# Expert stage of a recurrent/attention/MoE block: weight splits emitted four ahead, products with the weight's high part first

## The chip, the cores and the metric

One NeuronCore of one Trainium2 chip runs the whole block. The metric is device time in microseconds for one execution of the program. The kernel before takes 1919.03 us (median of 3 runs, 1914.31 to 1919.47); the one execution that was profiled took 1921.2 us, of which the trace spans 1919.1 us.

## The reference, cut to what matters

The block is an RWKV branch, a differential attention branch, a mix of the two, then a mixture of experts, then a gated per-layer term. The change touches the experts alone. Each of 1024 tokens goes to 2 of 32 experts; an expert is

```python
def expert_block(args):
    xb, e = args
    return (jax.nn.silu(xb @ w_gate[e]) * (xb @ w_up[e])) @ w_down[e]
```

with `w_gate` and `w_up` of 1024x512 and `w_down` of 512x1024, all in 32-bit floats. So each expert brings 6 MiB of weights and meets at most 128 rows of tokens in the main pass (an overflow loop behind it takes what is over 128).

## The kernel before, in words

A product of two 32-bit operands is built from three matmuls on rounded parts: each operand is split into a high part (`fp32r`, a copy on ScalarE) and a low part (the difference, on VectorE), and `mm3` (L69 to L73) issues high x high, high x low of the right operand, low x high, one after the other for each 128 rows of the contraction. In the experts the left operand is the tokens (`exh`, `exl`) or the activated rows (`eah`, `eal`), and the right operand, 512 columns wide, is the weight (`ewh`, `ewl`).

**Weights.** `weight_order` lists 192 pieces of 1 MiB, six for an expert: the upper half of gate and of up, then the two halves of down of the expert before, then the lower halves of gate and up. `wdma` (L1024) loads a piece on SyncE's queue into a ring of nine raw buffers (`ewp` five, `md` four). `wload` splits it, `ewh` on ScalarE (L78) and `ewl` on VectorE (L79), into a ring of four pairs (`wsp`, n = 4). So piece n+4 reuses the pair of piece n, and a load reuses the raw buffer of the load nine before it. Nine pieces are loaded before the stage starts.

**Experts.** For expert e the loop of `experts` gathers the tokens of e+1 (GpSimd, L1074), runs the first halves of gate and up (`expert_up`, PSUM tiles `pg`, `pu`), then `expert_down` of expert e-1, then the transposes and split of the next tokens (`expert_x`, `tp4` at L1064), then the second halves, then `expert_act`: Silu on ScalarE (L1097) and a product on VectorE (L1098). `expert_down` transposes the activated rows, splits them into `eah`, `eal`, multiplies by down into two PSUM tiles `pey`, copies these on ScalarE (L1117) and scatters the rows (GpSimd, L1118). `weight()` is a generator's step: a piece's split is written into the program right ahead of the matmuls that read it. `between` puts steps of the overflow's index work after each expert from the third on.

**Order.** The program is written in the order above, but a planner (`schedule_with_timeline_sim=True`) lays each engine's instructions out by a simulated timeline, with the place in the program as priority; on the chip each engine's order is then fixed. That is why the rows show `pg`, `pu` and `pey` matmuls interleaved.

Of the kernel before, what the change touches and what calls it, by code (L numbers as in the profile page):

```python
# [25 lines left out]
AF = mybir.ActivationFunctionType  # L26
# [6 lines left out]
D = 1024  # L33
NT = S // 128
KT = D // 128
# [9 lines left out]
NE = 32  # L45
FF = 512
# [6 lines left out]
class Kern:  # L53
    def __init__(self, ctx, tc, A, out, dbg=None):
        self.ctx, self.tc, self.nc, self.A, self.out = ctx, tc, tc.nc, A, out
        self.dbg = dbg or {}
        self.ovat = NE - 1
        self.flush = (NE - 1,)
        self.pre, self.bigat = (0, 1, 1, 1, 1, 1, 2, 2), 1
        self.nhold = 4  # L60
        self.w2seq = "sog sol sog l ogy l l l l"
        self.atn, self.w1gap, self.w1n, self.fln = 2.6, 3, 1.5, 0.6
# [1035 lines left out]
        self.nc.vector.tensor_mul(ac, ac, P[1])  # L1098
        return ac

    def expert_down(self, ac, rid, ws):

        ah = self.et("ah", [128, 4, 128], F32R)
        al = self.et("al", [128, 4, 128], F32R)
        self.split(ah, al, self.tp4(ac, 0))
        y = self.et("ye", [128, D])
        k = 0
        for hi, lo in ws:
            kn = hi.shape[1]
            for b in range(2):  # L1110
                cs = slice(b * 512, (b + 1) * 512)
                for i in range(kn):
                    self.mm3(self.pey[b], ah[:, k + i, :], al[:, k + i, :], hi[:, i, cs], lo[:, i, cs],
                             start=(k + i == 0), stop=(k + i == 3))
            k += kn
        for b in range(2):
            self.nc.scalar.activation(y[:, b * 512:(b + 1) * 512], self.pey[b], AF.Copy)  # L1117
        return self.nc.gpsimd.indirect_dma_start(out=self.yd, out_offset=bass.IndirectOffsetOnAxis(ap=rid, axis=0),  # L1118
                                                 in_=y, in_offset=None, bounds_check=2 * S - 1, oob_is_err=False)

    def weight_order(self):

        up, down, order = [], [], []
        for e in range(NE):
            wg, wu, wd = self.weights(e)
            up.append([(w, k, 4, FF) for k in (0, 4) for w in (wg, wu)])
            down.append([(wd, k, 2, D) for k in (0, 2)])
        for e in range(NE):
            order += up[e][:2]
            if e and e - 1 not in self.flush:  # L1130
                order += down[e - 1]
            order += up[e][2:]
            if e in self.flush:
                order += down[e]
        return order

    def experts(self, raws, between):

        order = self.weight_order()
        hold = {}  # L1140
        load = lambda n: self.wdma(*order[n], after=hold.get(n), sync=True)
        raws = list(raws)
        done = 0

        def weight():
            nonlocal done
            if not raws:
                raws.append(load(done))
            done += 1
            return self.wload(*order[done - 1], raws.pop(0))  # L1150

        sent, prev = [], None

        def down():
            e, ac = prev
            st = self.expert_down(ac, self.ids[:, 0, e:e + 1], (weight() for _ in range(2)))
            for s in sent:
                self.tc.declare_no_dep(st.ins, s.ins, reason="rows of other assignments")
            sent.append(st)
            self.lasty = st  # L1160

        gather = lambda e: self.expert_gather(self.ids[:, 1, e:e + 1])
        x = None
        for e in range(NE):
            if x is None:
                xg = gather(e)
                if not e:
                    hold.update({n: self.lastx for n in range(len(raws), len(raws) + self.nhold)})
                x = self.expert_x(xg)
            P = self.pgu[e % 2]  # L1170
            ahead = e < NE - 1 and e not in self.flush
            if ahead:
                xg = gather(e + 1)
            self.expert_up(x, P, (weight() for _ in range(2)), 0)
            if prev is not None:
                down()
            nx = self.expert_x(xg) if ahead else None
            self.expert_up(x, P, (weight() for _ in range(2)), 4)
            x = nx
            prev = e, self.expert_act(P)  # L1180
            if e in self.flush:
                down()
                prev = None
            between(e)

    def overflow_loop(self):
        nc, tc, A = self.nc, self.tc, self.A
        n = nc.values_load(self.ebi[0:1, 16:17], min_val=0, max_val=15)
        with tc.For_i(0, n, 1) as i:  # L1189
            e = nc.values_load(self.ebi[0:1, bass.ds(i, 1)], engines=[mybir.EngineType.SP],  # L1190
                               min_val=0, max_val=NE - 1)
            nc.vector.tensor_copy(self.idc, self.ido[:, :, bass.ds(i, 1)].rearrange("p a b -> p (a b)"))
            wg, wu, wd = [A[nm][0, bass.ds(e, 1)].rearrange("o k n -> (o k) n") for nm in ("w_gate", "w_up", "w_down")]
            x = self.expert_x(self.expert_gather(self.idc[:, 1:2]))
            for k in range(0, KT, 2):
                self.expert_up(x, self.pgu[0], (self.wload(w, k, 2, FF, pre="o") for w in (wg, wu)), k)
            self.expert_down(self.expert_act(self.pgu[0]), self.idc[:, 0:1],
                             (self.wload(wd, k, 1, D, pre="o") for k in range(4)))


    def ple_proj(self, pool):
# [358 lines left out]
```

## Time and profile before

| | |
|---|---|
| median of 3 runs | 1919.03 us |
| the profiled execution | 1921.2 us, span 1919.1 us |
| expert stage, first to last expert matmul | from 1168.6 to about 1795 us of the span |
| TensorE busy over the span | 93% |
| VectorE, ScalarE, GpSimd busy | 70%, 45%, 15% |
| granted TensorE clock over the span | 0.970 |

Busy shares are averages over stages with different limits; the expert stage is read by itself, with the waits in it. Matmuls are pipelined: one lasts about 0.40 us, but the next one starts before its end, so the pace is the distance of the starts. "PE" is a matmul, "PEld" the load of its left operand, and "SPq" SyncE's queue of loads. A wait is named by the engine and line that waited and by what released it.

### The profile page before, as it was taken

What the parts mean: (1) busy time and instruction counts of PE and PEld (TensorE: products, weight loads), DVE (VectorE), ACT (ScalarE), POOL (GpSimd) and SP (SyncE); (2) the same over time, 40 slices, a digit from 0 to 9 for tenths busy, and PEclk for the clock granted to TensorE, in tenths of its full rate; (3) what the DMA queues carried; (4) which work ended last, traced back from release to release, by engine and by line L of the source; (5) the groups of instructions that cost most, each with busy time, mean ns of one, the idle gap of its engine ahead of it and who ended that gap; (6) DMA issues with size and microseconds to landing.
All of it is one profiled execution on the core that took longest, in us unless ns stands there. A gap on an engine that the chain in (4) does not pass through costs nothing. (4 is left out here: it accounts for less than half of the span.)

```text
span 1919.1 us, 28589 instructions
## 1 busy us (share of the span) xinstructions
PE 1792.2 (93%) x10864; PEld 1486.9 (77%) x10864; DVE 1347.0 (70%) x2578; ACT 858.7 (45%) x1241; POOL 297.2 (15%) x211
## 2 busy tenths in 40 slices
PE   6999999999999988999988996999999999999598
PEld 6999898898766667888866875777777777777487
DVE  6455867743788937666555778998888787888673
ACT  5244444421333312122222226777767767777432
POOL 0311211000332310101042001222211121120000
PEclk9999999999999988899989997999999999999799
DMA  6432242237676565445354448999999999999641
GB/s 216 128 116 85 76 129 95 82 120 258 200 246 229 192 230 184 135 157 178 122 193 128 168 174 298 353 366 371 337 335 351 353 343 349 334 334 337 256 179 44
DMA packets 241789, 421.39 MB, mean 220 GB/s; under 512 B 38769, under 2 KB 115697, under 8 KB 240754
## 3 DMA queue, kind: packets, MB, share of 16 engines
q1 hardware_dynamic: 194546, 346.12, 52.8%
q10 hardware_dynamic: 37888, 56.64, 8.1%
q0 software_dynamic: 9216, 16.80, 2.4%
q8 instruction: 86, 1.41, 0.3%
q14 instruction: 53, 0.43, 0.1%
HBM read 346.07 MB, written 90.18 MB: 227 GB/s over the span
## 5 line engine op out<-in xcount | busy, mean ns | idle before, releaser
L79 DVE TENSOR_TENSOR ewl<-ewp,ewh 128x2048 fp32r<-128x2048 f32 x108 | 245.6, 2287 | 51.4 <-ACT ewh L78 50.9
L71 PE MATMUL pj<-whi,hh 128*128 128x256 f32 x832 | 239.8, 288 | 0.3 <-ACT pjev L208 0.3
L72 PE MATMUL pj<-wlo,hh 128*128 128x256 f32 x832 | 239.2, 288 | 0.0
L73 PE MATMUL pj<-whi,hl 128*128 128x256 f32 x832 | 237.4, 286 | 0.0
L79 DVE TENSOR_TENSOR ewl<-md,ewh 128x2048 fp32r<-128x2048 f32 x84 | 191.3, 2286 | 36.9 <-ACT ewh L78 36.5
L78 ACT ACTIVATE ewh<-ewp 128x2048 fp32r<-128x2048 f32 x108 | 204.6, 1910 | 11.4 <-PE pg L73 5.7
L71 PEld LDWEIGHTS pj<-whi,hh 128*128 128x128 f32 x832 | 159.2, 191 | 7.7 <-issue 6.6
L78 ACT ACTIVATE ewh<-md 128x2048 fp32r<-128x2048 f32 x84 | 159.1, 1911 | 11.5 <-PE pu L73 5.6
L72 PEld LDWEIGHTS pj<-wlo,hh 128*128 128x128 f32 x832 | 159.2, 191 | 6.2 <-issue 5.3
L73 PEld LDWEIGHTS pj<-whi,hl 128*128 128x128 f32 x832 | 159.0, 191 | 2.6 <-issue 2.3
L1074 POOL DMA_INDIRECT xg<-h2d,ids x32 | 64.0, 2000 | 402.0 <-PE ptp L1064 368.4
L72 PE MATMUL pu<-ewl,exh 128*128 128x512 f32 x256 | 105.1, 411 | 17.2 <-DVE ewl L79 17.2
L71 PE MATMUL pu<-ewh,exh 128*128 128x512 f32 x256 | 103.2, 403 | 3.6 <-ACT ewh L78 3.6
L72 PE MATMUL pey<-ewl,eah 128*128 128x512 f32 x256 | 100.8, 401 | 5.8 <-DVE ewl L79 5.8
L71 PE MATMUL pg<-hh,whi 128*128 128x512 f32 x256 | 105.2, 411 | 0.0
L72 PE MATMUL pg<-ewl,exh 128*128 128x512 f32 x256 | 103.0, 402 | 2.0 <-DVE ewl L79 2.0
L72 PE MATMUL pg<-hl,whi 128*128 128x512 f32 x256 | 103.9, 406 | 0.0
L71 PE MATMUL pg<-ewh,exh 128*128 128x512 f32 x256 | 103.2, 403 | 0.6 <-ACT ewh L78 0.6
L73 PE MATMUL pg<-hh,wlo 128*128 128x512 f32 x256 | 102.4, 400 | 0.0
L73 PE MATMUL pg<-ewh,exl 128*128 128x512 f32 x256 | 101.3, 396 | 0.0
L73 PE MATMUL pu<-ewh,exl 128*128 128x512 f32 x256 | 101.0, 394 | 0.0
L73 PE MATMUL pey<-ewh,eal 128*128 128x512 f32 x256 | 97.6, 396 | 0.2 <-DVE eal L79 0.2
(455 smaller groups left out, 4269.1 us busy)
## 6 DMA issues: line engine op xcount, KB each, us to landing
ewp<-in_w_down_dram SPq DMA_DIRECT2D x42, 1024.0 KB, 7.2
ewp<-in_w_gate_dram SPq DMA_DIRECT2D x33, 1024.0 KB, 7.3
ewp<-in_w_up_dram SPq DMA_DIRECT2D x33, 1024.0 KB, 7.9
md<-in_w_up_dram SPq DMA_DIRECT2D x31, 1024.0 KB, 7.4
md<-in_w_gate_dram SPq DMA_DIRECT2D x31, 1024.0 KB, 7.5
md<-in_w_down_dram SPq DMA_DIRECT2D x22, 1024.0 KB, 7.0
wraw<-in_w_in_dram SPq DMA_DIRECT2D x42, 512.0 KB, 4.0
gd<-pjev ACTq DMA_DIRECT2D x32, 256.0 KB, 4.8
```

What stands on the lines that cost most here:

```text
L71: mm(ps, lh, rh, start=start, stop=False)
L72: mm(ps, lh, rl, start=False, stop=False)
L73: mm(ps, ll, rh, start=False, stop=stop)
L78: a = nc.scalar.activation(hi, src, AF.Copy)
L79: b = nc.vector.tensor_tensor(lo, src, hi.bitcast(F32), op=OP.subtract)
L1074: self.lastx = self.nc.gpsimd.indirect_dma_start(out=xg, out_offset=None, in_=self.h2d, in_offset=bass.IndirectOffsetOnAxis(ap=tid, axis=0 ...
```

## The change

The split of a piece, and the load that feeds it, are now written four pieces ahead: four before the loop, then one (`more()`) after the matmuls of each piece. Inside a piece the matmuls with its high part (eight, tokens' high and low part in turn) come first, and the four with its low part last; in `expert_down` both column halves do their high products before the low ones. `expert_down` is cut in three: `expert_rows` (transposes and split of the activated rows) now stands between the first half of gate and the first half of up; the products stand where they were; `expert_out` (copies and scatter) stands after the second half of gate. Silu follows gate's second half at once. The order of the pieces and of their loads, the ring sizes and the number of matmuls are as before.

```diff
+        def more():
+            nonlocal done
+            if done < len(order):
+                raw = raws.pop(0) if raws else load(done)
+                ready.append(self.wload(*order[done], raw))
+                done += 1
+
+        def up(x, P, i, k0):
+            hi, lo = ready.pop(0)
+            mm = self.nc.tensor.matmul
+            for j in range(4):
+                for z in range(2):
+                    mm(P[i], x[z][:, k0 + j, :], hi[:, j, :], start=(k0 + j + z == 0), stop=False)
+            for j in range(4):
+                mm(P[i], x[0][:, k0 + j, :], lo[:, j, :], start=False, stop=(k0 + j == KT - 1))
+            more()
...
+        x = self.expert_x(xg)
+        for _ in range(4):
+            more()
         for e in range(NE):
...
-            self.expert_up(x, P, (weight() for _ in range(2)), 0)
-            if prev is not None:
-                down()
-            nx = self.expert_x(xg) if ahead else None
-            self.expert_up(x, P, (weight() for _ in range(2)), 4)
+            up(x, P, 0, 0)
+            if e:
+                a = self.expert_rows(ac)
+            up(x, P, 1, 0)
+            if e:
+                down(a)
+            nx = self.expert_x(xg) if e < NE - 1 else None
+            up(x, P, 0, 4)
+            ac = self.et("ac", [128, FF])
+            self.nc.scalar.activation(ac, P[0], AF.Silu)
+            if e:
+                out(e - 1)
+            up(x, P, 1, 4)
+            self.nc.vector.tensor_mul(ac, ac, P[1])
             x = nx
```

The products of down, with `a` the pair of split rows (`a[0]` high, `a[1]` low):

```diff
-        for hi, lo in ws:
-            kn = hi.shape[1]
-            for b in range(2):
-                cs = slice(b * 512, (b + 1) * 512)
-                for i in range(kn):
-                    self.mm3(self.pey[b], ah[:, k + i, :], al[:, k + i, :], hi[:, i, cs], lo[:, i, cs],
-                             start=(k + i == 0), stop=(k + i == 3))
-            k += kn
+        for b in range(2):
+            for i in range(kn):
+                for z in range(2):
+                    mm(self.pey[b], a[z][:, k + i, :], hi[:, i, half(b)], start=(k + i + z == 0), stop=False)
+        for b in range(2):
+            for i in range(kn):
+                mm(self.pey[b], a[0][:, k + i, :], lo[:, i, half(b)], start=False, stop=(k + i == 3))
```

## Rows read from the trace of the kernel before

**Rows 1.** Busy time by stage; columns: window, length, engines, clock, DMA share, GB/s.

```profile
1165.00:1345.00 180.00, 174.04 (x794) 139.96 (x795) 158.48 (x151) 132.88 (x112) 41.05 (x19) 0.98 0.99 358
1345.00:1790.00 445.00, 417.80 (x1909) 329.94 (x1907) 359.79 (x245) 317.38 (x270) 80.42 (x43) 1.00 0.96 341
...
1547.60:1626.90 79.30, 74.02 (x338) 58.49 (x337) 63.77 (x40) 57.04 (x49) 14.60 (x9) 1.00 0.97 344
```

**Rows 2.** Waits from 1345 to 1790 us: total us, times, longest.

```profile
DVE ewl L79 <- ACT ewh L78: 71.1, 55, 3.4
ACT eah L78 <- PE ptp L1064: 43.1, 22, 5.5
ACT eye L1117 <- PE pey L73: 34.5, 26, 2.8
ACT exh L78 <- PE ptp L1064: 31.6, 21, 3.9
PEld pu L72 <- DVE ewl L79: 24.2, 21, 1.8
...
PEld pey L72 <- DVE ewl L79: 9.1, 10, 1.8
...
PEld pg L72 <- DVE ewl L79: 5.0, 11, 1.3
...
PEld pey L71 <- ACT eah L78: 1.9, 3, 0.9
...
PEld pg L71 <- ACT ewh L78: 1.0, 1, 1.0
```

**Rows 3.** ScalarE's waits from 1165 to 1345 us.

```profile
ACT ewh L78 <- PE pu L73: 10.6, 15, 1.3
ACT ewh L78 <- PE pg L73: 10.4, 10, 3.8
```

**Rows 4.** Waits of SyncE's queue, 1200 to 1790 us.

```profile
SPq L1024 <- DVE ewl L79: 463.2, 164, 6.8
```

**Rows 5.** TensorE in order of time: a piece without a stall, then its end.

```profile
1375.01 0.40 PE L71 MATMUL pu<-ewh,exh 128*128 128x512 f32 x1
...
1377.81 0.60 PE L1064 MATMUL ptp<-ident,eac 128*128 128x128 f32 x4
```

**Rows 6.** TensorE in order of time: transposes, then a stall.

```profile
1494.51 0.60 PE L1064 MATMUL ptp<-ident,eac 128*128 128x128 f32 x4
1494.86 0.47 PE L71 MATMUL pu<-ewh,exh 128*128 128x512 f32 x1
1496.45 0.50 PE L72 MATMUL pu<-ewl,exh 128*128 128x512 f32 x1 [1.12 <-DVE ewl L79]
1496.79 0.40 PE L73 MATMUL pu<-ewh,exl 128*128 128x512 f32 x1
```

**Rows 7.** ScalarE in order of time around the same stall.

```profile
1491.67 0.60 ACT L78 ACTIVATE exh<-ptp 128x512 fp32r<-128x512 f32 x1 [2.23 <-PE pu L72]
1492.17 1.91 ACT L78 ACTIVATE ewh<-ewp 128x2048 fp32r<-128x2048 f32 x1
1495.14 0.60 ACT L78 ACTIVATE eah<-ptp 128x512 fp32r<-128x512 f32 x1 [1.07 <-PE ptp L1064]
```

**Rows 8.** VectorE in order of time around the same stall.

```profile
1494.10 2.29 DVE L79 TENSOR_TENSOR ewl<-ewp,ewh 128x2048 fp32r<-128x2048 f32 x1 [0.84 <-ACT ewh L78]
1496.32 0.68 DVE L79 TENSOR_TENSOR eal<-ptp,eah 128x512 fp32r<-128x512 f32 x1
```

**Rows 9.** DMA from 1300 to 1350 us: packets and rate, then one load's time to landing.

```profile
DMA packets 7996, 18.29 MB, mean 366 GB/s; under 512 B 644, under 2 KB 644, under 8 KB 7992
...
md<-in_w_gate_dram SPq DMA_DIRECT2D x2, 1024.0 KB, 12.0
```

**Rows 10.** DMA issues from 1345 to 1769 us: KB each, median us to landing.

```profile
ewp<-in_w_down_dram SPq DMA_DIRECT2D x29, 1024.0 KB, 7.2
```

**Rows 11.** SyncE's queue: the loads of down's halves, four experts apart.

```profile
1547.61 3.15 SPq L1024 DMA_DIRECT2D ewp<-in_w_down_dram  x2
...
1626.87 3.14 SPq L1024 DMA_DIRECT2D md<-in_w_down_dram  x2
```

**Rows 12.** The last expert's down: activated rows late.

```profile
1789.10 0.50 PE L71 MATMUL pey<-ewh,eah 128*128 128x512 f32 x1 [0.69 <-ACT eah L78]
...
1790.56 0.50 PE L73 MATMUL pey<-ewh,eal 128*128 128x512 f32 x1 [0.25 <-DVE eal L79]
```

**Rows 13.** GpSimd's gathers, from 1345 to 1790 us.

```profile
POOL xg L1074 <- PE ptp L1064: 258.3, 20, 16.2
```

More of the change, by code (lines that the diff above doesn't have):

```diff
@@ L56, in __init__ @@
         self.dbg = dbg or {}
-        self.ovat = NE - 1
-        self.flush = (NE - 1,)
         self.pre, self.bigat = (0, 1, 1, 1, 1, 1, 2, 2), 1
@@ L1099, in expert_act, with expert_rows @@
         return ac
-    def expert_down(self, ac, rid, ws):
+    def expert_rows(self, ac):
         ah = self.et("ah", [128, 4, 128], F32R)
@@ L1105, in expert_down, with expert_out @@
         self.split(ah, al, self.tp4(ac, 0))
-        y = self.et("ye", [128, D])
-        k = 0
-        for hi, lo in ws:
-            kn = hi.shape[1]
-            for b in range(2):
-                cs = slice(b * 512, (b + 1) * 512)
-                for i in range(kn):
-                    self.mm3(self.pey[b], ah[:, k + i, :], al[:, k + i, :], hi[:, i, cs], lo[:, i, cs],
-                             start=(k + i == 0), stop=(k + i == 3))
-            k += kn
+        return ah, al
+    def expert_down(self, a, w, k):
+        hi, lo = w
+        kn = hi.shape[1]
+        mm = self.nc.tensor.matmul
+        half = lambda b: slice(b * 512, (b + 1) * 512)
+        for b in range(2):
[5 more added lines that the diff above has]
+                mm(self.pey[b], a[0][:, k + i, :], lo[:, i, half(b)], start=False, stop=(k + i == 3))
+    def expert_out(self, rid):
+        y = self.et("ye", [128, D])
         for b in range(2):
@@ L1129, in weight_order @@
             order += up[e][:2]
-            if e and e - 1 not in self.flush:
+            if e:
                 order += down[e - 1]
             order += up[e][2:]
-            if e in self.flush:
-                order += down[e]
-        return order
+        return order + down[-1]
     def experts(self, raws, between):
@@ L1141, in experts, with down, out @@
         load = lambda n: self.wdma(*order[n], after=hold.get(n), sync=True)
-        raws = list(raws)
+        raws, ready, sent = list(raws), [], []
         done = 0
-        def weight():
+        def more():
             nonlocal done
[L1147 to L1156, printed above, removed]
+            if done < len(order):
[4 more added lines that the diff above has]
+            hi, lo = ready.pop(0)
+            mm = self.nc.tensor.matmul
+            for j in range(4):
[4 more added lines that the diff above has]
+            more()
+        def down(a):
+            for k in (0, 2):
+                self.expert_down(a, ready.pop(0), k)
+                more()
+        def out(e):
+            st = self.expert_out(self.ids[:, 0, e:e + 1])
             for s in sent:
@@ L1159, in down @@
             sent.append(st)
-            self.lasty = st
         gather = lambda e: self.expert_gather(self.ids[:, 1, e:e + 1])
-        x = None
-        for e in range(NE):
[L1165 to L1169, printed above, removed]
+        xg, ac = gather(0), None
+        hold.update({n: self.lastx for n in range(len(raws), len(raws) + self.nhold)})
+        x = self.expert_x(xg)
+        for _ in range(4):
+            more()
+        for e in range(NE):
             P = self.pgu[e % 2]
-            ahead = e < NE - 1 and e not in self.flush
-            if ahead:
+            if e < NE - 1:
                 xg = gather(e + 1)
-            self.expert_up(x, P, (weight() for _ in range(2)), 0)
-            if prev is not None:
-                down()
-            nx = self.expert_x(xg) if ahead else None
-            self.expert_up(x, P, (weight() for _ in range(2)), 4)
+            up(x, P, 0, 0)
[8 more added lines that the diff above has]
+            self.nc.scalar.activation(ac, P[0], AF.Silu)
+            if e:
+                out(e - 1)
+            up(x, P, 1, 4)
+            self.nc.vector.tensor_mul(ac, ac, P[1])
             x = nx
[L1180 to L1183, printed above, removed]
             between(e)
+        down(self.expert_rows(ac))
+        out(NE - 1)
     def overflow_loop(self):
@@ L1196, in overflow_loop @@
                 self.expert_up(x, self.pgu[0], (self.wload(w, k, 2, FF, pre="o") for w in (wg, wu)), k)
-            self.expert_down(self.expert_act(self.pgu[0]), self.idc[:, 0:1],
-                             (self.wload(wd, k, 1, D, pre="o") for k in range(4)))
+            a = self.expert_rows(self.expert_act(self.pgu[0]))
+            for k in range(4):
+                self.expert_down(a, self.wload(wd, k, 1, D, pre="o"), k)
+            self.expert_out(self.idc[:, 0:1])
     def ple_proj(self, pool):
```

## The prediction, made before the changed kernel ran

> **What bounds the kernel now.** I read the busy times by stage first. The expert stage has two parts. From 1165 to 1345 us TensorE is busy 174.0 of 180 us; from 1345 to 1790 us it is busy 417.8 of 445 us, with the clock at 1.00, that is at the upper level of 2.4 GHz [rows 1]. The second part is where time can be found. It repeats: down's loads return after 79.26 us for four experts, 19.8 us each [rows 11].
>
> Next the waits of that part. TensorE's loads wait 24.2 + 9.1 + 5.0 = 38.3 us for `ewl`, the low part of a weight, in 42 waits, all at L72, none longer than 1.8 us; 1.0 us goes to `ewh` and 1.9 us to `eah` [rows 2]. No row of TensorE names a DMA.
>
> Then the order of time, to see why a low part is late. The matmul before the stall starts at 1494.86, the one that needs `ewl` at 1496.45 [rows 6]. That `ewl` ran from 1494.10 to 1496.39 after VectorE had stood 0.84 us for its high part [rows 8]; the high part ran from 1492.17 on ScalarE, behind an `exh` for which ScalarE had stood 2.23 us until TensorE released it [rows 7]. ScalarE stands 43.1, 34.5 and 31.6 us in front of `eah`, `eye` and `exh`, and VectorE 71.1 us for `ewh` [rows 2]. So splits of weights queue behind small copies that wait for TensorE, and TensorE then waits for the split. In the first part ScalarE's waits in front of `ewh` are for a ring slot that the matmuls set free, 10.6 and 10.4 us [rows 3]: there the splits ran ahead, and TensorE hardly stalled.
>
> Last the transfers. SyncE's queue waits 463.2 us for `ewl`, the freeing of a raw buffer [rows 4]: loads wait for splits, not the reverse. A load issued nine pieces ahead has 9 x 79.3 / 24 = 29.7 us and lands in 7.2 us [rows 1, 10], some 22 us before it is needed.
>
> **The sum.** TensorE's own pace: twelve matmuls take 1377.81 - 1375.01 = 2.80 us [rows 5], so 72 take 16.8 us; four transposes take 0.35 us [rows 6] and lengthen the next distance by about 0.1 us, three such groups 1.3 us. That is 18.1 us for an expert, 72.4 us for four, against 79.3 [rows 1, 11]: 6.9 us lost, 1.7 us an expert. Over 22.5 experts (445 / 19.8) that is 38 us; the waits of rows 2 add up to 42.5 us with an `eac` wait at the end, so a microsecond of listed wait costs about 0.89 us.
>
> *High products first.* The first low product now comes after eight matmuls where it came after one: 7 x 0.233 = 1.63 us later. The 42 waits average 0.9 us and none is over 1.8 us [rows 2], so 38.3 x 0.89 = 34 us go, all but a few tenths. The number of matmuls is the same and each loads its left operand as before, so nothing is added there. High parts come free four matmuls, 0.93 us, before a piece's end, which lets the split four ahead begin earlier; the low part comes free 0.23 us later than now.
>
> *Splits four ahead.* With four ring slots, the split of piece n+4 cannot begin before the matmuls of n are done with the slot. The emission gives it a better place on ScalarE and VectorE, in front of `eah`, `exh`, `eye`, not an earlier possible start. It is what takes the `ewh` waits, 1.0 x 0.89 = 1 us, and keeps the splits from falling behind again as in rows 7. Loads are written earlier too, in the same order on SyncE; they still wait for the raw buffer, and what they are moved past are only their like. Together: 35 us off.
>
> *What is added.* `eah` and `eal` now stand behind a weight's split. Written out from a piece's end: `ewh` begins 0.93 us before it and takes 1.91 [rows 7], ends at 0.98; `eah` ends at 1.58; `ewl`, 2.29 [rows 8], from 0.98 to 3.27; `eal` to 3.95. TensorE does the transposes (0.43) and the next piece (2.80), and its second product of down, one place earlier than before, needs `eal` at 3.46. That is 0.5 us short per expert, nothing if the planner puts `eal` ahead. With ScalarE behind by one more copy and its rest (1.4 us) it is 1.9 us. Rows nearest: the last expert, with no cover, stalls 0.69 and 0.25 us there [rows 12]; today's `eah` waits are 0.1 us per expert [rows 2]. I take 0.2 us x 31 = 6 us, bounds 0 and 59.
>
> *Counted as nothing.* Silu's earlier place lies beside twelve matmuls of up. The scatter moves one piece later in GpSimd's queue, 2.8 us, and the gather behind it has 258.3 us in 20 waits for its buffer to spare [rows 13]. The four splits before the loop are those that fill the ring now. VectorE, busy 64 of 79.3 us [rows 1], would be busy 64 of about 73: it still fits, without much to spare.
>
> 35 - 6 = 29 us off the profiled execution: 1921.2 - 29 = 1892; that execution is 2 us over the median, so 1890 us.
>
> **Whether the transfers allow it.** From 1345 to 1790 us 341 GB/s x 445 us = 152 MB move [rows 1]. At the 366 GB/s of 1300 to 1350 us, where a load took 12.0 us to land [rows 9], they take 415 us, 30 us less, and the lead of 22 us can shrink besides. So 29 us passes, barely. The Trainium skill, page "DMA: Bandwidth & Descriptors", section "Where 436 GB/s comes from", speaks against it: for HBM to SBUF the HBM side, about 358 GB/s a core, is said to bind. By it the stretch could not fall under 424 us; this trace's 366 GB/s [rows 9] is above that figure already.
>
> **Rivals.**
> *The transfers become the bound.* If 358 GB/s, which the first part shows at a DMA share of 0.99 [rows 1], is all that lasts, 152 MB take 424 us: 21 us off, 1898 us. For it: a share of 0.96 already. Against it: 366 GB/s, and no wait of TensorE for a load.
> *The waits move and stay.* The ring still holds four; TensorE pulls ahead by 1.6 us and the splits, which start on its matmuls, come later by as much, held by the same copies. For it: ScalarE's 109 us before those copies [rows 2]. Against it: those waits are themselves for TensorE, and shorten with it. At most 5 us either way, 1914 to 1922 us.
> *The activated rows become the stall (slower).* If `eal` is 1.9 us late for every expert, 59 us come and 35 go: 24 us slower, 1943 us. It decides from 35 / 31 = 1.1 us an expert. For it: both splits in front in both queues, and the earlier need. Against it: TensorE's order is planned too, and can take low products first.
>
> **Chances.** Forecast (16 to 39 us off, 1880 to 1903 us; 39 is all of rows 2) 0.58; transfers 0.08, inside that range; moved waits 0.22, of which 0.13 within 0.3% and 0.09 a gain of 6 to 16 us; rows stall 0.12. A change of 0.3%, 5.8 us, is about the least that can be told here. Faster 0.75, same 0.13, slower 0.12. The range for 8 in 10 reaches from all stalls gone, 1878, to almost no change, 1916.
>
> **What would show it.** After: L72's waits for `ewl` a few us in all; expert period 18.1 to 18.6 us; GB/s above 355 with landings over 9 us. High-first is wrong if L72 still waits; the added term is wrong if `pey` waits for `eal` over 1 us an expert. A DMA named as what TensorE or ScalarE waits for would make the transfers the answer.

## Result and the profile after

The changed kernel takes 1898.71 us (median of 20 runs) where the kernel before takes 1916.4 us (20 runs): ratio 0.991, 95% interval 0.9896 to 0.9923, about 18 us. The profiled execution took 1893.14 us with a span of 1891.0 us, 28 us under the profiled one of before. That is more than the medians differ, and the first expert matmul shows why: it starts at 1157.96 us, before at 1168.57 us. Up to there every engine's instructions are the same in both programs, so 10.6 us of the 28 are spread between executions; nearly all of it arises between 770 and 870 us, and the granted clock from 600 to 900 us was 0.91 in the execution of before and 0.95 in this one. The 17.5 us that are left agree with the medians. From the first expert matmul to the start of the last, 626.5 us became 612.1 us, 14.4 us less; I call this stretch the stage. Some 3 us more went in the tail, which no experiment looked into.

Busy time by stage, columns as in [rows 1]: three experts of the repeating part, then the two parts of the stage.

```profile
1547.20:1604.50 57.30, 55.05 (x254) 43.72 (x252) 47.63 (x30) 42.56 (x37) 9.23 (x6) 1.00 0.99 353
1165.00:1345.00 180.00, 179.45 (x844) 145.64 (x842) 162.00 (x158) 138.30 (x118) 38.58 (x19) 1.00 1.01 369
1345.00:1750.00 405.00, 391.02 (x1791) 309.71 (x1790) 336.14 (x217) 298.79 (x252) 62.29 (x40) 1.00 0.98 353
```

Loads of down in time order, three experts apart:

```profile
1547.16 4.62 SPq L1022 DMA_DIRECT2D md<-in_w_down_dram  x2
...
1604.51 4.62 SPq L1022 DMA_DIRECT2D md<-in_w_down_dram  x2
```

57.35 / 3 = 19.1 us an expert (its period), against 19.8 in [rows 11] and 18.1 worked out for TensorE alone. So 0.7 us an expert came and 1.0 us did not. Where it stays is in the waits from 1345 to 1750 us:

```profile
ACT exh L76 <- PE ptp L1062: 55.9, 22, 3.2
DVE ewl L77 <- ACT ewh L76: 41.3, 46, 1.5
DVE eac L1201 <- PE pu L1164: 24.4, 18, 1.7
PEld pg L1164 <- DVE ewl L77: 19.0, 21, 1.3
...
PEld pu L1164 <- DVE ewl L77: 7.1, 38, 0.6
...
PEld pey L1118 <- DVE ewl L77: 1.5, 3, 0.6
```

TensorE waited 38.3 us for `ewl` in the 445 us of [rows 2], 1.7 us an expert, and 27.6 us in 405 us now, 1.3 us an expert, of which 19.0 us stand at one place: the low products of an expert's first gate piece, 21 times, once an expert. VectorE's wait in front of `eac`, the product of Silu and up, has grown to 24.4 us; before, from 1345 to 1790 us, it was

```profile
DVE eac L1098 <- PE pu L73: 7.5, 13, 0.7
```

In order of time after the change, VectorE first, then ScalarE, then TensorE:

```profile
1602.19 2.29 DVE L77 TENSOR_TENSOR ewl<-md,ewh 128x2048 fp32r<-128x2048 f32 x1 [1.45 <-ACT ewh L76]
1605.85 0.69 DVE L1201 TENSOR_TENSOR eac<-eac,pu 128x512 f32<-128x512 f32 x1 [1.36 <-PE pu L1164]
1606.45 2.28 DVE L77 TENSOR_TENSOR ewl<-md,ewh 128x2048 fp32r<-128x2048 f32 x1
```

```profile
1603.03 1.91 ACT L76 ACTIVATE ewh<-md 128x2048 fp32r<-128x2048 f32 x1
```

```profile
1607.44 0.60 PE L1062 MATMUL ptp<-ident,eac 128*128 128x128 f32 x4
1608.79 1.21 PE L1164 MATMUL pg<-ewl,exh 128*128 128x512 f32 x4 [0.75 <-DVE ewl L77]
```

VectorE stands 1.36 us until the last matmul of up lets the product go. The low part behind it, whose high part was ready at 1604.94, starts at 1606.45, ends at 1608.73, and TensorE's low products start at 1608.79, about 1.0 us later than the transposes before them would have allowed (1607.44 + 0.35). Begun at 1604.94, it would have ended by 1607.23, in time. That is the 1.0 us an expert.

### The profile page after: what moved, and what is told of

It reads as the page before. It is cut to its first block, busy times and chain, and to the rows that moved or that the text cites. A ratio compares the mean times of both kernels' runs of the same rounds, so it can differ in the third digit from the quotient of the medians.

```text
span 1891.0 us, 28588 instructions
## 1 busy us (share of the span) xinstructions
PE 1780.8 (94%) x10864; PEld 1478.0 (78%) x10864; DVE 1343.0 (71%) x2578; ACT 858.2 (45%) x1241; POOL 279.1 (15%) x211
## 5 line engine op out<-in xcount | busy, mean ns | idle before, releaser
L70 PE MATMUL pj<-wlo,hh 128*128 128x256 f32 x832 | 239.2, 288 | 0.0
L70 PEld LDWEIGHTS pj<-wlo,hh 128*128 128x128 f32 x832 | 159.2, 191 | 6.2 <-issue 5.3
L70 PE MATMUL pg<-hl,whi 128*128 128x512 f32 x256 | 103.8, 405 | 0.0
L1115 PE MATMUL pey<-ewh,eah 128*128 128x512 f32 x256 | 97.7, 401 | 0.7 <-ACT eah L76 0.7
L76 ACT ACTIVATE whi<-wraw 128x1024 fp32r<-128x1024 f32 x42 | 44.5, 1060 | 110.9 <-DMA wraw<-in_w_in_dram 60.8
L1164 PE MATMUL pg<-ewl,exh 128*128 128x512 f32 x256 | 72.5, 405 | 13.7 <-DVE ewl L77 13.4
```

The lines of the kernel that those rows point to most:

```text
L70: mm(ps, lh, rl, start=False, stop=False)
L76: a = nc.scalar.activation(hi, src, AF.Copy)
L1115: mm(self.pey[b], a[z][:, k + i, :], hi[:, i, half(b)], start=(k + i + z == 0), stop=False)
L1164: mm(P[i], x[0][:, k0 + j, :], lo[:, j, :], start=False, stop=(k0 + j == KT - 1))
```

## Experiments

My theory after the result: the order of the products brought the gain; splits emitted four ahead brought nothing that the times show, because in each engine's planned order they still run just before their use; what is left is VectorE standing in front of the Silu product. All were timed in five rounds beside the kernel before (medians 1914.91 us for the first four, 1915.33 us for the last three).

**One part alone: the order of the products.** In the kernel before:

```diff
...
-                self.mm3(ps, x[0][:, k, :], x[1][:, k, :], hi[:, i, :], lo[:, i, :],
-                         start=(k == 0), stop=(k == KT - 1))
+                for z in range(2):
+                    mm(ps, x[z][:, k0 + i, :], hi[:, i, :], start=(k0 + i + z == 0), stop=False)
+            for i in range(hi.shape[1]):
+                mm(ps, x[0][:, k0 + i, :], lo[:, i, :], start=False, stop=(k0 + i == KT - 1))
```

and down likewise.

> The kernel before with the order of the products alone: high part first, low part last, splits emitted where they were. Theory (the order of the products brought the gain, because the splits still finish just before they are used): ratio to before 0.988 to 0.994, expert period 19.0 to 19.3 us, listed waits of TensorE's loads for ewl under 25 us from 1345 us on. Rival (the emission four ahead brought it): ratio 0.997 to 1.0, period 19.6 to 19.8 us.

1902.62 us, ratio 0.991 (0.9881 to 0.9938): as much as the whole change. In the repeating part its loads of down return as often as after:

```profile
1559.24 4.62 SPq L1024 DMA_DIRECT2D md<-in_w_down_dram  x2
...
1616.55 4.61 SPq L1024 DMA_DIRECT2D md<-in_w_down_dram  x2
```

57.31 / 3 = 19.1 us. Its loads reach that pace later: those of down stand 20.0 us apart from 1381.88 to 1462.02 us (four experts). The stage is 613.1 us long, 1.0 us more than after. TensorE's loads wait 18.9 us for `ewl` from 1345 to 1740 us. VectorE's wait in front of the product comes with the order of the products alone (same stretch):

```profile
DVE eac L1100 <- PE pu L1095: 20.4, 16, 1.4
```

**The other part alone: splits four ahead.** The changed kernel with `mm3` back:

```diff
...
-            for j in range(4):
-                for z in range(2):
-                    mm(P[i], x[z][:, k0 + j, :], hi[:, j, :], start=(k0 + j + z == 0), stop=False)
-            for j in range(4):
-                mm(P[i], x[0][:, k0 + j, :], lo[:, j, :], start=False, stop=(k0 + j == KT - 1))
+            for j in range(4):
+                k = k0 + j
+                self.mm3(P[i], x[0][:, k, :], x[1][:, k, :], hi[:, j, :], lo[:, j, :],
+                         start=(k == 0), stop=(k == KT - 1))
```

> The changed kernel with the three matmuls of each row block in the order of before, so splits four ahead alone. Theory: the ring and the planner's order leave the splits just in time, so L72's kind of wait returns: ratio to before 0.997 to 1.003, period 19.6 to 19.9 us. Rival (emission ahead brought the gain): ratio 0.988 to 0.994, period 19.0 to 19.3 us.

1912.86 us, ratio 0.9994 (0.9975 to 1.0012): no difference that these runs show. (The stage of the one profiled execution is 622.6 us long, 3.9 us less than before; a gain of that size lies inside the interval.) Loads of down stand 19.9 us apart on average. The waits are again at the second matmul of a piece (L70 here is the L72 of before), from 1345 to 1740 us:

```profile
PEld pu L70 <- DVE ewl L77: 12.0, 12, 1.8
PEld pg L70 <- DVE ewl L77: 11.3, 10, 3.4
```

**The product behind the low part.** One edge of order for each expert in the changed kernel (it ties an instruction behind another on the same engine), where `lows` keeps each piece's `ewl` instruction and `ready[0]` is the next expert's first gate piece:

```diff
-            self.nc.vector.tensor_mul(ac, ac, P[1])
+            p = self.nc.vector.tensor_mul(ac, ac, P[1])
+            self.issue_after(p, lows[-len(ready)])
...
```

> The changed kernel with one edge of order more on VectorE: the Silu product of an expert is issued behind the low part of the next expert's first gate piece. Theory (the 1.0 us an expert that is left is VectorE standing in front of that product while a low part is due): period 18.1 to 18.6 us, ratio to before 0.975 to 0.984. Rival (transfers bind at 358 to 366 GB/s): period 18.6 to 19.0 us, and a wait of ScalarE for a DMA shows. Rival (the wait only moves, to the transposes of the product): period 19.0 to 19.3 us, ratio 0.99.

1882.56 us, ratio 0.9823 (0.9804 to 0.9843): the fastest version here, by the ratios about 17 us under the changed kernel and 34 us under before. VectorE now does the low part and then the product without standing in front of it:

```profile
1600.44 2.29 DVE L77 TENSOR_TENSOR ewl<-md,ewh 128x2048 fp32r<-128x2048 f32 x1 [0.49 <-ACT ewh L76]
1602.65 0.68 DVE L1203 TENSOR_TENSOR eac<-eac,pu 128x512 f32<-128x512 f32 x1
```

The wait at the first gate piece, 19.0 us to 1750 us in the changed kernel, is down to 4.7 us (1345 to 1740 us):

```profile
PEld pg L1166 <- DVE ewl L77: 4.7, 21, 0.6
```

What the edge changed in the engines' orders can be read from the two traces. From the first expert matmul on, ScalarE and GpSimd have the same order in both. On VectorE the product and the low part change places in 17 experts. On TensorE, where the planner answered, the four low products of the first gate piece stand in front of the transposes of the product 17 times, where they stood behind:

```profile
1602.90 1.09 PE L1166 MATMUL pg<-ewl,exh 128*128 128x512 f32 x4
1603.83 0.60 PE L1063 MATMUL ptp<-ident,eac 128*128 128x128 f32 x4
```

TensorE's new order alone could not have brought the gain: in the changed kernel those products started 0.06 us after their low part was done. The stage is 595.9 us long, 16.2 us under the changed kernel's 612.1, which is 0.95 us for each of the 17 experts.

Its loads of down and its stage from 1345 to 1740 us:

```profile
1545.24 3.15 SPq L1023 DMA_DIRECT2D md<-in_w_down_dram  x2
...
1599.97 3.15 SPq L1023 DMA_DIRECT2D md<-in_w_down_dram  x2
```

```profile
1345.00:1740.00 395.00, 393.77 (x1815) 311.78 (x1814) 342.93 (x225) 304.19 (x255) 66.26 (x40) 1.00 1.00 365
```

54.73 / 3 = 18.2 us an expert, 0.1 us over TensorE's own 18.1; TensorE is busy 393.8 of 395 us. The transfers run at 365 GB/s and do not bind: no wait of TensorE, ScalarE or VectorE names a DMA from 1345 to 1740 us, and SyncE's queue still waits for splits.

```profile
SPq L1023 <- DVE ewl L77: 328.9, 125, 4.7
```

**Splits really ahead, by order.** The order of ScalarE and VectorE fixed to the program's by edges, each block's small work in front of the split that follows it:

```diff
...
             up(x, P, 0, 0)
             if e:
                 a = self.expert_rows(ac)
+            more()
             up(x, P, 1, 0)
+            more()
...
+            self.queue(None, self.nc.vector.tensor_mul(ac, ac, P[1]))
+            more()
```

`queue` ties each instruction behind the one before on its engine; splits, rows, tokens, Silu and copies go through it.

> The changed kernel with the order on ScalarE and VectorE in the experts fixed by edges to the order of the program, small work of a block (rows, tokens, Silu, copies, product) in front of the split that follows the block. Theory (a split that is really four ahead needs the engines' order, which the planner did not give): splits finish two or more pieces before use, period 18.1 to 18.6 us, ratio 0.975 to 0.984. Rival (transfers bind): splits wait for loads, ScalarE or VectorE idle until a DMA, period 18.6 to 19.1 us. Rival (rows stall at eal): pey waits 0.5 us or more an expert for eal, period 18.6 to 20 us.

1911.71 us, ratio 0.9979 (0.9965 to 0.9994); loads of down 19.3 us apart, the stage 629.7 us long. The theory was nearly right about the splits: in the steady part low parts end 4.2 to 6.4 us (one and a half to two pieces) before their first use, against 0.05 to 1.2 us in the changed kernel, and no wait of TensorE for `ewl` is left. Its time failed, and the second rival's period came: the rows stall, though more at `eah` (0.9 us an expert) than at `eal` (0.4, where 0.5 was named). Waits from 1345 to 1740 us:

```profile
ACT eah L77 <- PE ptp L1071: 83.5, 20, 5.9
...
PEld pey L1124 <- ACT eah L77: 18.0, 20, 0.9
...
PEld pey L1124 <- DVE eal L78: 8.1, 19, 0.4
```

The planner put the transposes of the product late in TensorE's order, so ScalarE stands 4 us an expert in front of `eah` with three splits behind it, and the first products of down wait 0.9 and 0.4 us for the rows. Fixing two engines' order left the third free to answer. Whether a split truly ahead with a good order on all three would do better was not tried; the experiment before leaves 0.1 us an expert for it.

**Without the product.** The product of Silu and up is left out (down reads Silu alone), nothing else:

```diff
-            self.nc.vector.tensor_mul(ac, ac, P[1])
```

> The changed kernel without the product of Silu and up on VectorE (that product is left out of the computation; down reads Silu alone), no edge added. Theory (VectorE standing in front of this product is what makes the first gate piece's low part late): period 18.1 to 18.5 us, ratio to before 0.976 to 0.985, waits of pg for ewl under 6 us from 1345 us on. Rival (ScalarE's order makes it late, the product only stands near): period 18.9 to 19.2 us, ratio 0.989 to 0.992.

1884.79 us, ratio 0.9823 (0.979 to 0.9855), loads of down 18.5 us apart. The `pg` wait goes from 19.0 us (to 1750 us) to 3.1 us; what is left is spread over three places (1345 to 1740 us):

```profile
PEld pey L1118 <- DVE ewl L77: 8.4, 19, 0.6
...
PEld pu L1164 <- DVE ewl L77: 6.3, 20, 0.3
PEld pg L1164 <- DVE ewl L77: 3.1, 19, 0.2
```

This fits the theory but does not by itself separate it from the rival, because the planner also laid out ScalarE's, VectorE's and TensorE's orders differently in many places here. The run with the edge does separate them: it has ScalarE's order unchanged and the wait down to 4.7 us. So it is the product in front of the low part, not ScalarE's order, that made the low part late.

**The edge with splits two ahead.** Four becomes two in the version with the edge:

```diff
-        for _ in range(4):
+        for _ in range(2):
             more()
```

> The changed kernel with the edge of order (Silu product behind the low part of the next first gate piece), but splits emitted two pieces ahead where there were four. Theory (how far ahead a split is emitted does not set when it runs): period 18.2 to 18.4 us, ratio to before 0.979 to 0.986. Rival (the place in the program counts once the product is out of the way): period 18.6 us or more, ratio over 0.986.

1889.18 us, ratio 0.986 (0.9835 to 0.9886); its interval overlaps that of four ahead. The theory's period came, its ratio just. The repeating part has the same 18.2 us:

```profile
1551.52 3.15 SPq L1023 DMA_DIRECT2D md<-in_w_down_dram  x2
...
1606.22 3.15 SPq L1023 DMA_DIRECT2D md<-in_w_down_dram  x2
```

but it gets there later: its loads of down are still 20 us apart from 1375.15 to 1435.95 us, where four ahead has 18.2 to 18.7 from 1398.86 us on, and its stage is 602.9 us long against 595.9. So in these two executions the distance of emission counts in the stretch ahead of the steady pace, and not in the steady part; why it counts there was not looked into.

**The edge with the old order of products.** `mm3` back, as in the second experiment, edge kept (diffs as there).

> The edge of order and splits four ahead, but the three matmuls of each row block in the order of before. Theory (low parts are finished just in time, so the late low products are needed too): the second matmul of a piece waits for ewl as before, period 19.2 to 19.8 us, ratio 0.992 to 1.0. Rival (the edge alone is enough): period 18.2 to 18.6 us, ratio 0.980 to 0.986.

1910.35 us, ratio 0.997 (0.9949 to 0.9991). Its period is 19.9 us, just over the theory's 19.8. The waits are nearly those of the second experiment (1345 to 1740 us):

```profile
PEld pu L70 <- DVE ewl L77: 12.0, 12, 1.8
PEld pg L70 <- DVE ewl L77: 11.0, 8, 3.4
```

Every engine has the same order of instructions through the experts as in the second experiment, and the stage is 622.6 us long in both: with low products second, the planner already puts the product behind that low part, and the edge changes nothing. So 0.9994 and 0.997 are two measurements of one order, and a difference of 0.0024 between two experiments is not an effect by itself. With the edge, the order of the products is worth the step from 0.997 to 0.9823.

## Why the prediction was right, and where its size was off

The time, 1898.71 us, lies in the forecast range of 1880 to 1903 us and the direction was right; 29 us were forecast and about 18 came.

- *High products first, 34 us:* the mechanism holds. Alone it gives ratio 0.991, and once the remaining stall is out of the way the change gives the whole of this term and the next: 1914.91 x (1 - 0.9823) = 34 us against the 35 us of the sum. How the 34 us divide between the two is open: with the edge and splits two ahead it was 1915.33 x (1 - 0.986) = 27 us, and the edge without emission ahead was not run. TensorE's pace of 18.1 us an expert, worked out from two rows, was reached within 0.2 us. That the changed kernel alone fell short is the third term.
- *Splits four ahead, 1 us and "a better place on ScalarE and VectorE":* the better place did not come. Alone the emission is worth nothing that the times show (0.9994), and low parts still end just before their use (1608.73 for 1608.79). Emission is a wish to the planner, not an order on the engine. It helps in the stretch ahead of the steady pace at most (1.0 us of stage between the first experiment and after; 7 us between two and four ahead).
- *What is added, 6 us:* this is the term that was mis-sized. I priced the queue in front of `eal`, where 0.2 us an expert was taken; after, no matmul waits for `eal` there in the list. The wait that came is one step earlier, at the product that makes the rows: VectorE stands 1.36 us for the end of up and the next first gate piece's low part, behind it, costs TensorE 1.0 us an expert. It comes with the order of the products alone, not with the new places of the splits. Taking this wait away gives 16 us, so the term was about 16 us, not 6. On VectorE the prediction asked only what stands behind the split (`eal`), and not what the split stands behind (the product).
- *Transfers:* the rival's 1898 us is almost the measured time, but by coincidence: the changed kernel moved 353 GB/s, and without the stall the transfers ran at 365 GB/s for 395 us and neither TensorE nor the splits waited for them. The sentence of the Trainium skill that the prediction cites (page "DMA: Bandwidth & Descriptors", section "Where 436 GB/s comes from"), that the HBM side at about 358 GB/s binds for HBM to SBUF, does not hold for this run; the measurement decides.
- *The waits move and stay:* in part this came. Of the 1.7 us of listed wait an expert 1.3 are still there, mostly at another place. But what holds the split is the product on VectorE, where this rival named the copies on ScalarE: with ScalarE's order unchanged the edge took the wait away.
- *Rows stall, the slower rival:* not in the changed kernel, but its mechanism is real: with ScalarE's and VectorE's order fixed the rows cost 0.9 + 0.4 us an expert in waits, and nearly the whole gain was gone.
- *What would show it:* period 18.1 to 18.6 us was missed (19.1); L72's waits "a few us in all" was missed (27.6 us, at one place for the most part); over 355 GB/s with landings over 9 us was missed (353 GB/s, loads of down landing in 7.1 us). `pey` did not wait for `eal`, so the added term was not where it was looked for.

## What to carry to other kernels

Where an operand arrives in two parts, use first what is ready first: putting eight matmuls, where there was one, in front of those that need the late part hid waits that emitting the work earlier left in place. When a wait is removed, look on the engine that produces for the next instruction that stands in front of it: here one product that waited for TensorE held back a split that did not, and one edge of order an expert gave about as much again as the whole change. Read what an engine's order is in the trace before counting on a place in the program.

## Hardware seen here that was not expected

In the version with the edge and splits four ahead, one core's DMA moved 365 GB/s over 395 us at a DMA share of 1.00, while a 1 MiB load still landed in about 8 us (1345 to 1740 us):

```profile
ewp<-in_w_down_dram SPq DMA_DIRECT2D x28, 1024.0 KB, 7.9
```

At 341 GB/s it was 7.2 us [rows 1, 10]: a share near 1.00 in the profile was not yet a wait for transfers.
